# Expert activations of a two-layer decoder trunk: one 512-column and one 256-column matmul per K chunk, halves joined by adding DMAs

## The chip, the cores and the metric

One core of one Trainium2 chip runs the whole kernel. The metric is the device time of one execution in microseconds (us). The median of three runs of the kernel before is 2028.8 us (2027.66 to 2029.06).

## What is computed

The trunk has two layers over 256 tokens of width 1024. Layer 0 mixes tokens with a state-space block, layer 1 with attention; after each mixer comes a layer norm, a product-key expert block (PEER), another layer norm and a gated embedding add. The change touches only the expert block, which the reference writes as a gather:

```
u_g = u[expert]
v_g = v[expert]
act = jax.nn.gelu(jnp.einsum('td,thkd->thk', xb, u_g).astype(f32))
return jnp.einsum('thk,thkd->td', (gate * act).astype(v_g.dtype), v_g)
```

There are 16,384 experts per layer, `u` and `v` hold one row of 1024 numbers for each, and every token picks 128 of them (8 heads, 16 each). All data are float32.

## The kernel before, in words

The kernel does not gather. For each layer it computes the activation of **every** expert for every token, multiplies it by a gate that is zero for experts that a token did not pick, and multiplies the result by `v`. The 16,384 experts are handled as 128 groups of 128; the code calls a group `e`, and from here on "expert" means such a group.

**Precision.** The matmuls of the experts take operands in a rounded float32 format (float32r). So each operand is split into a high part (a cast on ScalarE, ACT) and a low part (the difference, on VectorE, DVE), and each product is made of three: high·high, high·low and low·high (`SPLIT`, L29). `split` (L112) is the pair of instructions, L113 the cast and L114 the difference.

**Weights.** `chunk` (L117) loads one 128x1024 float32 tile of 512 KB into a `raw` buffer by a DMA issued from SyncE (SP, L124), and splits it into an `hl` tile. There are three `raw` buffers (L110) and four `hl` buffers (L120).

**The u stage** (`expert_in`, L796). `stationary` (L140) goes over eight K chunks of 128. For each it calls `mm3` (L136): three matmuls whose stationary operand is a 128x128 piece of the weights (high, high, low) and whose moving operand is 256 tokens of the transposed activations `xT` (high, low, high). So an expert is 24 matmuls of 256 columns. Two experts share one 128x512 bank of PSUM (tag `mm`, two banks, L98), and after the second ACT applies Gelu to the whole bank and writes it to SBUF (L803), into one of four `act` tiles of 32 experts each.

**The v stage** (`expert`, L860). The gated activations of an expert are split into `w`, its `v` tile into `hl`, and 12 matmuls of 512 columns (2 token blocks x 2 column halves x 3) add into four PSUM banks (tag `acc`, four banks, L101) over all 128 experts.

**Order of the work.** The instruction order on each engine is fixed when the program is built. `weave` (L40) spreads a list of side steps over a list of main steps, so that VectorE's routing and gating work lies between the loads of the experts. In a layer the u stage runs with three kinds of company: two experts among the queries (L865 to L871); experts 2 to 71 with `route`, the top-16 searches and lookups on VectorE (L873); experts 72 to 127 with the first half of the gating (L874). The v stage runs its first 62 experts with the second half of the gating, `second` (L876). The gating builds one-hot tiles (L815 to L821), multiplies them on TensorE (L830) and multiplies the result into `act` (`weigh`, L837). Towards the end of the v stage the 512 KB tiles of the next projection (`w_pg`) are loaded among the experts (L891).

GpSimd (POOL) has almost nothing to do and issues no DMA.

Of the kernel before, what the change touches and what calls it, by code (L numbers as in the profile page):

```python
# [7 lines left out]
F32 = mybir.dt.float32  # L8
# [3 lines left out]
AF = mybir.ActivationFunctionType  # L12
OP = mybir.AluOpType
# [4 lines left out]
P = 128  # L18
T = 256
D = 1024  # L20
KD = D // P
# [36 lines left out]
class Net:  # L58
# [48 lines left out]
        return self.ps.tile([P, 512], F32, tag="aux", bufs=2, name=self.name("aux"))  # L107

    def raw(self):
        return self.stream.tile([P, 1024], F32, tag="raw", bufs=3, name=self.name("raw"))  # L110

    def split(self, hi, lo, src, lo_on=None):  # L112
        a = self.nc.scalar.copy(hi, src)  # L113
# [16 lines left out]
    def plain(self, src):  # L130
        raw = self.raw()
        dma = self.nc.sync.dma_start(raw, src)
        self.pace.marks = (dma.ins,)
        return raw
# [5 lines left out]
    def stationary(self, out, hl, m=P):  # L140
        for k in range(KD):
            self.mm3(out, lambda a: hl[:, a, k * m:(k + 1) * m], lambda b: self.xT[:, b, k, :],
                     k == 0, k == KD - 1)

    def moving(self, out, hl, xk, first, last, c=slice(0, 512)):
        for k in range(2):
            self.mm3(out, lambda a: xk(a, k), lambda b: hl[:, b, k * 512 + c.start:k * 512 + c.stop],
                     first and k == 0, last and k == 1)
# [4 lines left out]
    def load_xT(self, j):  # L153
        raw = self.xT32[:, 2 * j:2 * j + 2, :].rearrange("p k t -> p (k t)")
        self.nc.sync.dma_start(raw, self.dram["xT"][j])
        f = lambda a: self.xT[:, a, 2 * j:2 * j + 2, :].rearrange("p k t -> p (k t)")
        self.split(f(0), f(1), raw)
# [179 lines left out]
    def tl(self, shape, tag, bufs, dt=F32):  # L337
        return self.pool.tile(shape, dt, tag=tag, bufs=bufs, name=self.name(tag))
# [319 lines left out]
    def peer(self, i):  # L658
        nc, dram = self.nc, self.dram
        with self.tc.tile_pool(name=f"peer{i}", bufs=1) as pool:  # L660
            self.pool = pool
            tl = lambda shape, dt, tag, bufs=1: self.tl(shape, tag, bufs, dt)
# [130 lines left out]
            act = {}  # L793
            cur = {}

            def expert_in(e):  # L796
                if e % 32 == 0:
                    act[e // 32] = tl([P, 32, T], F32, f"act{e // 32}")
                if e % 2 == 0:
                    cur["ph"] = self.mm().rearrange("p (e t) -> p e t", e=2)  # L800
                self.stationary(cur["ph"][:, e % 2], self.chunk(dram["u"][i, e]))
                if e % 2:
                    nc.scalar.activation(act[e // 32][:, e % 32 - 1:e % 32 + 1, :], cur["ph"], AF.Gelu_apprx_tanh)  # L803

            gw = {}

# [33 lines left out]
            def gating(half):  # L840
                steps = []
                for tg in range(0, 32, 2):
                    steps += [lambda tg=tg: pick(half, tg), lambda tg=tg: pick(half, tg + 1),
                              lambda tg=tg: spread((tg, tg + 1)),
                              lambda tg=tg: weigh(half, tg), lambda tg=tg: weigh(half, tg + 1)]
                return steps
# [3 lines left out]
            def expert_load(e, w=None, hl=None):  # L850
                w = tl([P, 2, T], F32R, "w", 3) if w is None else w
                self.split(w[:, 0, :], w[:, 1, :], act[e // 32][:, e % 32, :])
                return w, self.chunk(dram["v"][i, e], hl=hl)

            def expert_out(e, w, hl, tb):
                for h in range(2):
                    self.mm3(accs[tb][h], lambda a: w[:, a, tb * P:(tb + 1) * P],
                             lambda b: hl[:, b, h * 512:(h + 1) * 512], e == 0, e == 127)

            def expert(e):  # L860
                w, hl = expert_load(e)
                for tb in range(2):
                    expert_out(e, w, hl, tb)

            for hc in range(19):  # L865
                if hc < 16:
                    query(hc)
                elif hc < 18:
                    expert_in(hc - 16)
                if hc >= 3:  # L870
                    score(hc - 3)  # L871
            first, second = gating(0), gating(1)
            self.weave([lambda e=e: expert_in(e) for e in range(2, 72)], route)  # L873
            self.weave([lambda e=e: expert_in(e) for e in range(72, 128)], first)  # L874
            accs += self.accs()
            self.weave([lambda e=e: expert(e) for e in range(62)], second)  # L876
            self.weave([lambda e=e: expert(e) for e in range(62, 90)], [])
            res = tl([P, 4, 2, D], F32, "act1")
            x, gb0, gb1, pp = (res[:, k] for k in range(4))
# [163 lines left out]
```

## Time and profile before

| | |
|---|---|
| median of 3 runs | 2028.8 us |
| profiled execution, its own time | 2027.79 us |
| span of the profile (first to last instruction) | 2026.0 us |
| granted TensorE clock | 1.00 throughout |
| TensorE, weight loads | 1817.5 us busy (90%), 14,706 of them |
| DMA queue of SP | 367.29 MB, 56.1% of 16 engines |
| u stage of layer 0 / layer 1 | about 283 to 660 us / 1248 to 1625 us |
| v stage of layer 0 / layer 1 | about 660 to 1023 us / 1625 to 1990 us |

How to read it: all durations in the groups come from that one profiled execution, which took 2027.79 us by its own clock, 1.8 us more than the span. A line such as `L113 ACT CAST hl<-raw ... x626 | 654.8, 1047` says that the instructions of line 113 on ACT were 626, busy for 654.8 us in all, 1047 ns each on average. A matmul's duration is its whole way through the array, and neighbours overlap, so the time that one costs is read from how many fit in a stretch of the chain of waits. In the rows by windows, each row is a stretch of the span, then its length, then the busy time of each engine in it with the number of instructions, the granted clock, and the DMA engines' busy share and rate.

### The profile page before, as it was taken

Reading aid. Unit: us, or ns where it says so; the run is one execution under the profiler, and the core shown is the slowest. Engines: PE = TensorE matmul, PEld = TensorE weight load, DVE = VectorE, ACT = ScalarE, POOL = GpSimd, SP = SyncE. Lnnn points to the kernel's source line nnn. Section 1 sums busy time; section 2 is a strip of 40 time slices with the busy share of each in tenths; the row PEclk is TensorE's granted clock in tenths of the full one; section 3 lists DMA queues with packets and bytes.
Section 4 is the critical chain, followed back from the end, with each engine's and each line's share of the span. In section 5 each row is a group of like instructions: output and inputs, shape, how many; then the busy total and the mean of one; then the engine's idle time right before and its main releaser. Section 6 shows DMA issues by size and latency. Waiting matters only on the chain.

```text
span 2026.0 us, 36796 instructions
## 1 busy us (share of the span) xinstructions
PE 2001.7 (99%) x14706; PEld 1817.5 (90%) x14706; DVE 1553.3 (77%) x3050; ACT 1010.6 (50%) x1472; POOL 26.4 (1%) x31
## 2 busy tenths in 40 slices
PE   9999999999999999999999999999999999999998
PEld 8888899999999888888879889999999988888887
DVE  8786659997777988866665655999787888986665
ACT  6754544455444444445545654445544444445553
POOL 0001000000000000000000000000000000000000
PEclk9999999999999999999999999999999999999999
DMA  7446655555555555666745555555555555566672
GB/s 270 156 133 197 210 174 181 179 184 184 159 173 161 176 167 187 226 209 201 235 138 177 177 179 165 186 179 187 175 161 175 159 178 175 178 214 221 201 227 83
DMA packets 102732, 369.64 MB, mean 182 GB/s; under 512 B 11392, under 2 KB 12320, under 8 KB 100896
## 3 DMA queue, kind: packets, MB, share of 16 engines
q1 hardware_dynamic: 102560, 367.29, 56.1%
q8 instruction: 115, 1.88, 0.4%
q14 instruction: 57, 0.47, 0.1%
HBM read 360.92 MB, written 6.32 MB: 181 GB/s over the span
## 4 chain that ended last, share of the span: by engine, by line
PE 79%; issue 8%; DMA 5%; DVE 5%; ACT 2%; POOL 1%; SPq 0%; POOLq 0%; ACTq 0%
PE mm L138 42%; PE acc L138 31%; DMA raw<-in_v 3%; PE aux L830 3%; DVE hl L114 2%; ACT hl L113 1%; DVE cv_y L351 1%; DMA raw<-in_w_pg 1%; PE aux L689 1%; PE aux L456 0%; DMA raw<-in_w_xbc 0%; PE mm L166 0%; PE mm L371 0%; DMA raw<-in_w_q 0%; POOL sq L477 0%
## 5 line engine op out<-in xcount | busy, mean ns | idle before, releaser
L138 PE MATMUL mm<-xT,hl 128*128 128x256 f32 x8112 | 1003.4, 284 | 1.8 <-DVE hl L114 1.1
L138 PEld LDWEIGHTS mm<-xT,hl 128*128 128x128 f32 x8112 | 981.5, 192 | 6.3 <-issue 2.0
L114 DVE TENSOR_TENSOR hl<-raw,hl 128x1024 fp32r<-128x1024 f32 x624 | 758.6, 1221 | 282.3 <-ACT hl L113 280.2
L113 ACT CAST hl<-raw 128x1024 fp32r<-128x1024 f32 x626 | 654.8, 1047 | 291.6 <-PE mm L138 174.2
L138 PE MATMUL acc<-hl,w 128*128 128x512 f32 x3024 | 697.5, 391 | 1.5 <-DVE hl L114 0.7
L138 PEld LDWEIGHTS acc<-hl,w 128*128 128x128 f32 x3024 | 564.7, 188 | 120.7 <-DVE hl L114 2.3
L113 ACT CAST w<-act 128x256 fp32r<-128x256 f32 x252 | 101.9, 406 | 269.0 <-PE acc L138 261.1
L803 ACT ACTIVATE act<-mm 128x512 f32<-128x512 f32 x128 | 76.5, 598 | 227.6 <-PE mm L138 227.4
L114 DVE TENSOR_TENSOR w<-act,w 128x256 fp32r<-128x256 f32 x252 | 106.0, 421 | 43.7 <-ACT w L113 42.9
L837 DVE SCALAR_TENSOR_TENSOR act<-aux,act 128x256 f32<-128x256 f32 x256 | 90.5, 416 | 26.0 <-PE aux L830 26.0
L821 DVE TENSOR_TENSOR a<-oh,r 128x512 f16<-128x512 f16 x256 | 96.3, 417 | 0.0
L815 DVE TENSOR_TENSOR oh<-iota,r 128x1024 f16<-128x1024 f16 x128 | 87.2, 682 | 0.0
L830 PEld LDWEIGHTS <-oh 128*128 128x128 f16 x2048 | 63.3, 98 | 9.7 <-issue 8.4
L830 PE MATMUL aux<-a,oh 128*128 128x64 f16 x2048 | 70.9, 193 | 0.0
L817 DVE TENSOR_TENSOR oh<-iota,r 128x512 f16<-128x512 f16 x128 | 53.3, 417 | 0.0
L138 PE MATMUL acc<-hl,nhl 128*128 128x512 f32 x192 | 49.2, 407 | 0.0
L138 PEld LDWEIGHTS acc<-hl,nhl 128*128 128x128 f32 x192 | 34.8, 188 | 9.8 <-issue 1.0
L138 PE MATMUL acc<-act,xT 128*128 128x512 f32 (+1 forms) x186 | 40.8, 373 | 0.0
L138 PEld LDWEIGHTS acc<-act,xT 128*128 128x128 f32 x186 | 32.2, 189 | 5.6
L351 DVE SCALAR_TENSOR_TENSOR cv_y<-cv_raw,params,cv_y 128x253 f32<-128x253 f32 (+2 forms) x72 | 34.4, 486 | 2.3 <-ACT cv_y L348 1.8
L727 DVE MAX8 act<-act 128x8 f32<-128x128 f32 (+1 forms) x96 | 32.1, 334 | 2.3
L114 DVE TENSOR_TENSOR act<-raw,act 128x1024 fp32r<-128x1024 f32 x16 | 19.6, 1226 | 16.3 <-ACT act L113 16.2
(213 smaller groups left out, 1048.7 us busy)
## 6 DMA issues: line engine op xcount, KB each, us to landing
raw<-in_u SPq DMA_DIRECT2D x256, 512.0 KB, 3.6
raw<-in_v SPq DMA_DIRECT2D x256, 512.0 KB, 4.3
raw<-in_w_q SPq DMA_DIRECT2D x32, 512.0 KB, 4.5
raw<-in_w_xbc SPq DMA_DIRECT2D x24, 512.0 KB, 3.7
raw<-in_w_z SPq DMA_DIRECT2D x16, 512.0 KB, 3.5
raw<-in_w_so SPq DMA_DIRECT2D x16, 512.0 KB, 4.4
raw<-in_w_pg SPq DMA_DIRECT2D x16, 512.0 KB, 4.5
raw<-in_w_qk SPq DMA_DIRECT2D x16, 512.0 KB, 3.9
```

Of the source, the lines that this page charges most:

```text
L113: a = self.nc.scalar.copy(hi, src)
L114: b = (lo_on or self.nc.vector).tensor_tensor(lo, src, hi.bitcast(F32), op=OP.subtract)
L138: self.nc.tensor.matmul(out, lhs(a), rhs(b), start=start and i == 0, stop=stop and i == 2)
L351: nc.vector.scalar_tensor_tensor(y[:, d:], raw[:, :T - d], w(k), y[:, d:], op0=OP.mult, op1=OP.add)
L689: nc.tensor.matmul(pss[:, tb], q[:, tb * P:(tb + 1) * P], keys[:, hc, :], start=True, stop=True)
L727: nc.vector.max(vals[:, 8:], src)
L803: nc.scalar.activation(act[e // 32][:, e % 32 - 1:e % 32 + 1, :], cur["ph"], AF.Gelu_apprx_tanh)
L815: nc.vector.tensor_tensor(pairs(oh2), every(self.iota, P), twins(i2T, P), op=OP.is_equal)
L817: nc.vector.tensor_tensor(pairs(oh1), every(self.iota[:, 64 * half:64 * half + 64], 64), twins(i1T, 64), op=OP.is_equal)
L821: nc.vector.tensor_tensor(pairs(a2[:, k]), pairs(oh1), twins(g2[:, k], 64), op=OP.mult)
L830: nc.tensor.matmul(pg[:, t, :], oh2[:, t], a2[:, k, t], start=k == 0, stop=k == 1)
L837: nc.vector.scalar_tensor_tensor(v, pg[:, :, 32 * a:32 * a + 32].rearrange("p t e -> p e t"), 2.0 ** -12, v, op0=OP.mult, op1=OP.mult)
```

## The change

For each K chunk of an expert, two matmuls take the place of three. The first has the high part of the weights as its stationary operand and 512 moving columns: the high parts of the 256 tokens and then their low parts, which lie 8 KB apart in each partition of `xT`. The second has the low part of the weights and 256 columns, the high parts, and adds into the first half of the bank. So the bank holds high·high + low·high in its first half and high·low in its second. An expert has a bank of its own, of tag `acc`.

ACT copies the first half into `act` and the second into a new tile `low` (three buffers of two experts). After each second expert GpSimd issues a DMA that adds `low` (256 KB, from SBUF) onto the two experts in `act` (SBUF). Gelu is applied in place in SBUF to four experts at a time, 128x1024, and is ordered on ACT behind the copies of the expert that ends the next four; the last four follow inside the v stage, as the fourth side step of `second`. `raw` gets a fourth buffer, and the space that is reserved in SBUF for the descriptors of GpSimd's DMAs is set to 4096 bytes per partition.

```diff
     def raw(self):
-        return self.stream.tile([P, 1024], F32, tag="raw", bufs=3, name=self.name("raw"))
+        return self.stream.tile([P, 1024], F32, tag="raw", bufs=4, name=self.name("raw"))
...
+    def halves(self, out, hl):
+        o = out.rearrange("p (b t) -> p b t", b=2)
+        for k in range(KD):
+            c = slice(k * P, (k + 1) * P)
+            self.nc.tensor.matmul(o, hl[:, 0, c], self.xT[:, :, k, :], start=k == 0, stop=False)
+            self.nc.tensor.matmul(out[:, :T], hl[:, 1, c], self.xT[:, 0, k, :], start=False, stop=k == KD - 1)
...
+            def gelu(e):
+                x = act[e // 32][:, e % 32:e % 32 + 4, :].rearrange("p e t -> p (e t)")
+                nc.scalar.activation(x, x, AF.Gelu_apprx_tanh)
+
             def expert_in(e):
                 if e % 32 == 0:
                     act[e // 32] = tl([P, 32, T], F32, f"act{e // 32}")
                 if e % 2 == 0:
-                    cur["ph"] = self.mm().rearrange("p (e t) -> p e t", e=2)
-                self.stationary(cur["ph"][:, e % 2], self.chunk(dram["u"][i, e]))
+                    cur["low"] = tl([P, 2, T], F32, "low", 3)
+                pe = self.acc()
+                self.halves(pe, self.chunk(dram["u"][i, e]))
+                nc.scalar.copy(act[e // 32][:, e % 32, :], pe[:, :T])
+                copied = nc.scalar.copy(cur["low"][:, e % 2, :], pe[:, T:]).ins
                 if e % 2:
-                    nc.scalar.activation(act[e // 32][:, e % 32 - 1:e % 32 + 1, :], cur["ph"], AF.Gelu_apprx_tanh)
+                    both = act[e // 32][:, e % 32 - 1:e % 32 + 1, :]
+                    nc.gpsimd.dma_start(both, cur["low"], accum_op=OP.add)
+                if e % 4 == 3 and e > 3:
+                    with self.after((copied,)):
+                        gelu(e - 7)
...
             accs += self.accs()
+            second.insert(3, lambda: gelu(124))
             self.weave([lambda e=e: expert(e) for e in range(62)], second)
...
-    nc = bacc.Bacc("TRN2", target_bir_lowering=False, num_devices=1)
+    nc = bacc.Bacc("TRN2", target_bir_lowering=False, num_devices=1, dynamic_dma_scratch_size=4096)
```

## The prediction

> **What bounds the kernel now.** I read the page first, then the chain of waits in order of time, then the stages by windows, then the groups and waits of the u stage.
>
> ```profile
> PE 2001.7 (99%) x14706; PEld 1817.5 (90%) x14706; DVE 1553.3 (77%) x3050; ACT 1010.6 (50%) x1472; POOL 26.4 (1%) x31
> ...
> PE 79%; issue 8%; DMA 5%; DVE 5%; ACT 2%; POOL 1%; SPq 0%; POOLq 0%; ACTq 0%
> ```
>
> TensorE is busy for 99% of the span and carries 79% of the chain that ended last. A busy matmul is not yet a matmul that costs time, so the next view is the chain in order of time, in pieces of so many matmuls (start, length, what):
>
> ```profile
> 283.66 198.71 PE mm L138 x1656
> ...
> 846.38 119.82 PE acc L138 x528
> ...
> 1248.07 198.71 PE mm L138 x1656
> ```
>
> The first and third rows are 69 experts of the u stage of each layer without a break: 198.71 us / 1656 = 120.0 ns for a matmul of 256 columns. The second is 44 experts of the v stage: 119.82 / 528 = 226.9 ns for 512 columns. Doubling the columns adds 106.9 ns, so 256 columns cost 106.9 ns of streaming and each matmul about 13.1 ns besides, whatever its size. In these stretches TensorE never waits, so the u stage is as long as its matmuls. The rows of the routing and gating stretches say how far the others are from taking over:
>
> ```profile
> core 0: us, PE busy (x) PEld busy (x) DVE busy (x) ACT busy (x) POOL busy (x), PEclk, DMA share, GB/s
> ...
> 283.00:482.00 199.00, 199.00 (x1661) 199.00 (x1661) 182.18 (x494) 100.25 (x118) 0.00 (x0) 1.00 0.58 183
> 482.00:660.00 178.00, 178.00 (x1857) 177.31 (x1856) 139.92 (x248) 74.42 (x91) 0.00 (x0) 1.00 0.53 166
> ...
> 293.00:373.00 80.00, 80.00 (x669) 80.00 (x668) 74.75 (x242) 35.51 (x43) 0.00 (x0) 1.00 0.59 185
> 373.00:433.00 60.00, 60.00 (x502) 60.00 (x501) 59.28 (x160) 26.87 (x31) 0.00 (x0) 1.00 0.55 176
> 433.00:463.00 30.00, 30.00 (x252) 30.00 (x251) 27.72 (x53) 22.27 (x27) 0.00 (x0) 1.00 0.64 194
> ```
>
> VectorE is the one to watch: 182.18 of 199 us beside the routing, and 59.28 of 60 us in its densest part. ACT, the DMA engines and, above all, POOL (no instruction) have room.
>
> **The change part by part.**
>
> *TensorE.* Per K chunk 3 x 120.0 = 360.0 ns become 226.9 + 120.0 = 346.9 ns: the columns stay the same, 768, and one matmul's fixed 13.1 ns goes. Per expert 8 x 13.1 = 0.105 us, for 256 experts 2048 x 13.1 ns = 26.8 us. All of it lies on the path. The new matmul's moving operand comes in two runs of 256, which no matmul of this kernel does now; the bounds are 226.9 ns (the row of 512 columns in one run) and 2 x 120.0 = 240.0 ns (as if each run were a matmul of its own), that is 26.8 us or nothing. I take 226.9, as the row nearest in columns and in instructions; the other end is a rival.
>
> [...]
>
> *ACT.* The groups that give its prices (busy, mean ns, then idle before and what ended it); the last two are of the size of the new Gelu and of the new copies:
>
> ```profile
> L114 DVE TENSOR_TENSOR hl<-raw,hl 128x1024 fp32r<-128x1024 f32 x69 | 83.9, 1215 | 11.7 <-ACT hl L113 11.2 <-PE mm L138 0.5
> ...
> L113 ACT CAST hl<-raw 128x1024 fp32r<-128x1024 f32 x69 | 72.1, 1045 | 42.5 <-PE mm L138 38.7 <-DMA raw<-in_u 3.8
> L803 ACT ACTIVATE act<-mm 128x512 f32<-128x512 f32 x35 | 20.9, 597 | 54.6 <-PE mm L138 54.5
> L755 ACT COPY act<-act 128x1024 f16<-128x1024 f16 x8 | 8.0, 1044 | 0.0
> ...
> L690 ACT COPY act<-aux 128x256 f32<-128x256 f32 x2 | 0.7, 370 | 0.0
> ```
>
> For two experts ACT now does 0.60 us of Gelu and 2 x 1.05 of casts, 2.69 us in 5.76. After: four copies of 0.37, two casts, and half a Gelu of 128x1024, priced like the cast and L755 at 1.05: 1.48 + 2.09 + 0.52 = 4.09 us in 5.55. It fits, off the path. What it moves is the time at which the high part of a later expert is cast. The row of L113 shows that cast waiting for TensorE for 38.7 us: it is issued when an expert's matmuls end and free one of four `hl` tiles, so TensorE has three experts in hand, 8.3 us, while cast (1.05) and difference on VectorE (1.22) follow. The copies delay it by 0.74 us, every fourth time by a Gelu more. Cover remains, so I cost it at nothing; without that cover it would be 0.74 to 1.8 us per expert.
>
> One stretch is tight. From 433 to 463 us ACT is busy for 22.27 of 30 us. In the same experts, 10.4 of them, it gets 5.2 x (4.09 - 2.69) = 7.3 us more, 29.6 in the 28.9 us that TensorE then takes. Just before it, from 373 to 433 us, VectorE has 59.28 us of work where TensorE will take 60 x 346.9/360 = 57.8. Together that is 0.7 + 1.5 = 2.2 us per layer by which helpers fall behind; three experts in hand can absorb it, down to nothing lost. Bounds: 0 to 2.2 us per layer; I take 1, so 2 us.
>
> *The wait that is added.* Gelu of four experts stands on ACT's queue and waits for the adding DMA; behind it are the next copies and casts, for them VectorE's differences, and for these TensorE. It stands behind the copies of the expert that ends the next four, so the younger of the two DMAs has 4 x 2.78 = 11.1 us from its issue. No DMA of this kernel adds or is issued by POOL. The nearest rows are moves of 256 KB (KB each, then us from issue to landing); the load of an expert and the whole queue stand beside them:
>
> ```profile
> raw<-in_u SPq DMA_DIRECT2D x256, 512.0 KB, 3.6
> ...
> q1 hardware_dynamic: 102560, 367.29, 56.1%
> ...
> act<-in_keys SPq DMA_DIRECT2D x8, 256.0 KB, 5.2
> ...
> x_d<-xn SPq DMA_DIRECT2D x4, 256.0 KB, 2.6
> ```
>
> They land 2.6 to 5.2 us after issue. Even twice the longer is 10.4 us, inside the 11.1, and behind these come the 8.3 us that TensorE has in hand; so I cost the wait at nothing at both ends, as long as the DMA engines keep up (a rival). POOL's queue holds nothing else in these stages (0.00, x0), and SP's queue is not touched by the adds. The engine time: 367.29 MB are 56.1% of 2026 us, so all 16 engines together move 323 GB/s, and a plain 256 KB costs 0.81 us. Loads take 2 x 524 KB / 323 = 3.25 us of the 5.55 us of two experts; 2.3 us are free, 2.8 times a plain copy.
>
> *The last four.* Their Gelu comes in the v stage, where ACT reaches it as soon as the fourth expert's cast is issued, about when the u stage ends; its adding DMA lands 0.74 us of copies and 2.6 to 5.2 us later, and 8.2 us of v matmuls are in hand. The v stage's four banks are now those of the last four experts of the u stage; the last of the four is first written 9 x 0.227 = 2.0 us into the stage and its copies take 0.74. I take 0.5 us per layer for the seam, 1 us in all; bounds 0 and 2.
>
> *The fourth `raw` buffer.* It matters where a load ends a wait, at the end of the v stage with the extra `w_pg` tiles:
>
> ```profile
> 966.00:1064.00 98.00, 96.42 (x436) 78.38 (x435) 63.03 (x88) 47.82 (x67) 2.05 (x3) 1.00 0.59 183
> ...
> 1909.00:2007.00 98.00, 95.68 (x420) 76.97 (x419) 63.77 (x88) 51.36 (x71) 1.09 (x2) 1.00 0.59 183
> ...
> 968.98 4.68 DMA raw<-in_v
> 976.03 4.31 DMA raw<-in_v
> ```
>
> The last two rows are from the chain of waits: there the path runs from load to load, about 7 us for three buffers. But TensorE idles in these two stretches for only 1.58 + 2.32 = 3.9 us, part of it behind a layer norm. I take 2 us of gain, bounds 0 and 4.
>
> *Sum.* -26.8 - 2 + 2 + 1 = -25.8 us against the profiled execution's 2027.79: 2002.0. That execution lies 1.0 us below the median of the runs, so the forecast for the median is **2003 us**, 1.3% less.
>
> **The rivals.**
>
> *The DMA engines become the bound (slower).* [...] If it costs twice a plain copy, 1.6 us, it fits in the 2.3 us that are free. It decides from 5.76 - 3.25 = 2.5 us on, 3.1 times a plain copy: then two experts take longer than the 5.76 us of now, loads come late and ACT stands at Gelu or TensorE at a bank. At four times, 3.25 us, two experts take 6.5 us: 128 x 0.74 = 95 us more, about 2124 us. For it: an addition is done on the way and nothing here shows its rate. Against it: the margin of nearly three. Chance 0.14.
>
> *VectorE and ACT take over beside the routing (half a gain).* For it: 59.28 of 60 us and ACT's 29.6 in 28.9. In the row of L114 above VectorE stands waiting for ACT's cast for 11.2 us of that stage, with the routing queued behind it. If the later casts double these, VectorE needs 182.18 + 11.7 + 11.2 = 205 us for a stage that TensorE would do in 192: the stage ends 13 us later than forecast, less what 8.3 us in hand cover, 5 us per layer. 2003 + 10 = 2013 us. Against it: a VectorE that is behind no longer waits for casts. Chance 0.12.
>
> *Nothing is saved on TensorE.* If each of the two runs costs as much as a matmul, the 26.8 us stay: 2028.8 + 1, about 2030 us, no change. Against it: nothing in the trace points to a cost of a second run. Chance 0.06.
>
> **How the numbers follow.** Forecast 0.68, helpers 0.12, nothing saved 0.06, DMA bound 0.14. The forecast's own range is 1994 to 2009: below, the stalls at nothing (-3), all of the 3.9 us (-2) and another 4 us where the chain's 5% of DMA waits lie in other stages; above, their upper bounds (2.4 more at the routing, 1 at the seam, 2 for `raw`). Two of ten may be left out, so the range reaches over the helpers' case and as far beyond it, to 2023. About 0.2%, 4 us, is what a measurement of this kernel can tell from no change. Faster: 0.68 + 0.12 = 0.80; same 0.06; slower 0.14.
>
> **What would show it.** In the chain after, the u stage stands as unbroken pieces of 16 matmuls per expert, 2.78 us each instead of 2.88; 1656 matmuls of two layers' routing stretch become 1104 in about 191.5 us each. The new 512-column form steps at 227 ns; 240 would prove the third rival. Adding DMAs land within 5 us or so, DMA share in the u stage rises from 0.58 to 0.75 or 0.9, and Gelu waits for none of them; a Gelu that waits for a DMA and a share near 1 would prove the first. Casts of `raw` at the end of the v stage should wait less for loads. The forecast is wrong if the u stages don't shrink by 13 us each.

## The result and the profile after

The kernel after takes 1997.4 us (median of 6 runs, 1996.32 to 1998.53), the kernel before 2028.2 us beside it (6 runs, 2026.55 to 2029.35): a ratio of 0.9848, interval 0.9837 to 0.9859. That is 30.8 us less, where the forecast had 25.8. The profiled execution after took 1996.32 us by its own clock, the lowest of its six, with a span of 1994.4 us against 2026.0. The total is near the forecast. Two of its terms are not, as the stages show.

From the page of the kernel after: busy time, the two DMA queues with packets, MB and share, the shares of the chain, three groups of ACT and POOL, and two rows of DMA issues.

```profile
PE 1977.0 (99%) x12658; PEld 1706.0 (86%) x12658; DVE 1549.8 (78%) x3050; ACT 1138.1 (57%) x1920; POOL 135.4 (7%) x159
...
q1 hardware_dynamic: 102560, 367.29, 55.4%
q0 software_dynamic: 18432, 33.56, 9.9%
...
PE 85%; issue 7%; DVE 5%; ACT 2%; POOL 1%; DMA 1%; SPq 0%; POOLq 0%; ACTq 0%; DVEq 0%
...
L814 ACT COPY act<-acc 128x256 f32<-128x256 f32 x256 | 96.2, 376 | 254.2 <-PE acc L150 254.2
...
L815 ACT COPY low<-acc 128x256 f32<-128x256 f32 x256 | 98.2, 384 | 0.0
...
L805 ACT ACTIVATE act<-act 128x1024 f32<-128x1024 f32 x64 | 69.0, 1078 | 0.8 <-DMA act<-low 0.8
...
raw<-in_u SPq DMA_DIRECT2D x256, 512.0 KB, 4.4
...
act<-low POOLq DMA_DIRECT2D x128, 256.0 KB, 5.5
```

TensorE has the 2048 matmuls less (14,706 - 12,658). Gelu (L805) stood idle for an adding DMA for 0.8 us in the whole run. An adding DMA lands 5.5 us after its issue and costs 9.9% x 1994.4 / 128 = 1.54 us of all 16 engines, 1.9 times the 0.81 us worked out for a plain copy. What in it costs the time is not shown. DMA has gone from 5% of the chain to 1%; the forecast's term for it was 2 us.

Where the time went is read from landmarks in the chain of waits (start, length, what). Before: the first layer norm, the first v matmuls of layer 0, their last two pieces, the next layer norm, and the same for layer 1.

```profile
212.38 3.53 DVE xn L189 x2
...
663.39 8.19 PE acc L138 x36
...
1023.56 6.87 PE acc L138 x29
1030.87 1.39 PE acc L138 x6
...
1178.70 2.86 DVE x L189
...
1627.80 8.19 PE acc L138 x36
...
1996.72 1.39 PE acc L138 x6
```

After:

```profile
208.82 3.55 DVE xn L196 x2
...
649.77 8.19 PE acc L138 x36
...
832.76 181.01 PE acc L138 x798
1014.21 1.39 PE acc L138 x6
...
1160.65 2.92 DVE x L196
...
1600.99 8.20 PE acc L138 x36
...
1784.00 181.01 PE acc L138 x798
1965.45 1.39 PE acc L138 x6
```

The differences of these starts, in us:

| stretch | before | after | change |
|---|---|---|---|
| start to first layer norm | 212.4 | 208.8 | -3.6 |
| norm to v stage, layer 0 (holds the u stage) | 451.0 | 440.9 | -10.1 |
| v stage, layer 0 | 367.5 | 364.4 | -3.0 |
| attention, to the norm of layer 1 | 147.8 | 146.4 | -1.4 |
| norm to v stage, layer 1 (holds the u stage) | 449.1 | 440.3 | -8.8 |
| v stage, layer 1 | 368.9 | 364.5 | -4.5 |
| rest | 29.3 | 29.0 | -0.3 |

The u stages gave 18.8 us, not 26.8 (23.8 with the stalls that were forecast); the other stages, where of the change only the fourth buffer and the last Gelu of a layer lie, gave 12.8 us, not 2. The last 798 matmuls of each v stage now run without a break, at 181.01 / 798 = 226.8 ns. Two questions follow: why a buffer was worth so much, and where 8 us of the u stages went.

### The profile page after: what moved, and what is told of

Its sections match the earlier page's. It is cut to its first block, busy times and chain, and to the rows that moved or that the text cites. A ratio compares the mean times of both kernels' runs of the same rounds, so it can differ in the third digit from the quotient of the medians.

```text
span 1994.4 us, 33756 instructions
## 1 busy us (share of the span) xinstructions
PE 1977.0 (99%) x12658; PEld 1706.0 (86%) x12658; DVE 1549.8 (78%) x3050; ACT 1138.1 (57%) x1920; POOL 135.4 (7%) x159
## 4 chain that ended last, share of the span: by engine, by line
PE 85%; issue 7%; DVE 5%; ACT 2%; POOL 1%; DMA 1%; SPq 0%; POOLq 0%; ACTq 0%; DVEq 0%
PE acc L138 38%; PE acc L149 21%; PE acc L150 11%; PE mm L138 8%; PE aux L848 3%; DVE hl L114 1%; PE aux L696 1%; PE mm L378 1%; ACT hl L113 0%; PE aux L463 0%; PE mm L173 0%; DVE act L732 0%; PE mm L291 0%; DVE act L733 0%; DVE act L735 0%
## 5 line engine op out<-in xcount | busy, mean ns | idle before, releaser
L149 PE MATMUL acc<-xT,hl 128*128 128x512 f32 x2048 | 722.4, 397 | 0.0
L150 PE MATMUL acc<-xT,hl 128*128 128x256 f32 x2048 | 573.9, 280 | 0.4 <-DVE hl L114 0.4
L149 PEld LDWEIGHTS acc<-xT,hl 128*128 128x128 f32 x2048 | 384.8, 188 | 88.6
L150 PEld LDWEIGHTS acc<-xT,hl 128*128 128x128 f32 x2048 | 387.4, 189 | 1.1 <-DVE hl L114 1.1
L138 PE MATMUL mm<-xT,hl 128*128 128x256 f32 x1968 | 256.4, 287 | 0.8 <-DVE xT L114 0.7
L138 PEld LDWEIGHTS mm<-xT,hl 128*128 128x128 f32 x1968 | 242.3, 192 | 5.0 <-issue 2.3
L814 ACT COPY act<-acc 128x256 f32<-128x256 f32 x256 | 96.2, 376 | 254.2 <-PE acc L150 254.2
L818 POOL DMA_DIRECT2D act<-low x128 | 110.5, 863 | 758.5 <-ACT low L815 619.4
L815 ACT COPY low<-acc 128x256 f32<-128x256 f32 x256 | 98.2, 384 | 0.0
L805 ACT ACTIVATE act<-act 128x1024 f32<-128x1024 f32 x64 | 69.0, 1078 | 0.8 <-DMA act<-low 0.8
L193 POOL TENSOR_TENSOR ln_s<-ln_s,mhalf 128x1 f32<-128x1 f32 x8 | 4.4, 549 | 874.3 <-DVE ln_s L192 874.3
```

The lines of the kernel that those rows point to most:

```text
L138: self.nc.tensor.matmul(out, lhs(a), rhs(b), start=start and i == 0, stop=stop and i == 2)
L149: self.nc.tensor.matmul(o, hl[:, 0, c], self.xT[:, :, k, :], start=k == 0, stop=False)
L150: self.nc.tensor.matmul(out[:, :T], hl[:, 1, c], self.xT[:, 0, k, :], start=False, stop=k == KD - 1)
L814: nc.scalar.copy(act[e // 32][:, e % 32, :], pe[:, :T])
L815: copied = nc.scalar.copy(cur["low"][:, e % 2, :], pe[:, T:]).ins
L818: nc.gpsimd.dma_start(both, cur["low"], accum_op=OP.add)
```

## The experiments

### raw4_only: the fourth buffer alone

```diff
 (kernel before)
-        return self.stream.tile([P, 1024], F32, tag="raw", bufs=3, name=self.name("raw"))
+        return self.stream.tile([P, 1024], F32, tag="raw", bufs=4, name=self.name("raw"))
...
-    nc = bacc.Bacc("TRN2", target_bir_lowering=False, num_devices=1)
+    nc = bacc.Bacc("TRN2", target_bir_lowering=False, num_devices=1, dynamic_dma_scratch_size=4096)
```

> The kernel before with the fourth raw buffer and the 4096 bytes of descriptor space alone. Theory 1, read from the two traces: the gain of 30.8 us is two gains, about 18.8 us in the two u stages (the matmuls) and about 12.5 us outside them (3.6 before the first norm, 3.0 and 4.5 in the v stages, 1.4 in the attention), and the second comes from the fourth buffer alone. Then this kernel is 12 us faster than the kernel before, ratio 0.994. Theory 2, the sizes of the prediction: the buffer is worth 2 us, at most 4, ratio 0.998 to 0.999, and the rest comes with the new matmuls.

Measured: 2016.2 us (5 runs, 2015.11 to 2016.65), ratio 0.9943, interval 0.993 to 0.9957: 12 us less than before. Its chain at the same landmarks:

```profile
209.16 3.55 DVE xn L189 x2
...
659.44 8.19 PE acc L138 x36
...
842.43 181.01 PE acc L138 x798
1023.88 1.39 PE acc L138 x6
...
1170.14 2.93 DVE x L189
...
1620.68 8.19 PE acc L138 x36
...
1985.12 1.39 PE acc L138 x6
```

The same steps as in the table: -3.2 to the first norm, -0.7, -3.0 in the v stage (364.4), -1.6, +1.4, and -4.5 in the second v stage (364.4). The v stages, the first mixer and the attention come out as in the kernel after to within 0.4 us. So the buffer alone explains what lies outside the u stages, and its gain lies in four stages, of which the prediction had looked at two, the v stages.

### raw3: everything but the fourth buffer

```diff
 (kernel after)
-        return self.stream.tile([P, 1024], F32, tag="raw", bufs=4, name=self.name("raw"))
+        return self.stream.tile([P, 1024], F32, tag="raw", bufs=3, name=self.name("raw"))
```

> The changed kernel with three raw buffers. Theory 1: only the u stages are shorter, by 18 to 19 us together, ratio 0.991. Theory 2: the matmuls give the 26.8 us of the prediction less 2 or 3 of stalls, ratio 0.988. If three buffers are too few for loads beside the adding DMAs, TensorE waits for loads in the u stage and less than 15 us are left.

Measured: 2007.0 us (4 runs, 2003.51 to 2008.25), ratio 0.9894, interval 0.9879 to 0.9909: 21.1 us less than before. The chain of its v stage goes from load to load again. In its profiled execution, the slowest of the four, the u stages (442.7 and 440.5 us between the landmarks) are 16.9 us shorter than before; the two v stages (366.5 and 365.8 us) are 4.1 us shorter, for which the runs show no cause. The total lies between the two theories, and its interval, 18.5 to 24.5 us, does not part them. 12.0 + 21.1 is 2.3 us more than the 30.8 of both; that interval covers this too.

### no_add: without the adding DMAs

```diff
                 if e % 2:
                     both = act[e // 32][:, e % 32 - 1:e % 32 + 1, :]
-                    nc.gpsimd.dma_start(both, cur["low"], accum_op=OP.add)
+                    pass
```

The high·low part stays out of the activations here.

> The changed kernel without the 128 adding DMAs: the high x low part of each activation is computed and copied, but left out of the result. Theory 1: the adds are hidden, so the time is that of the changed kernel within 2 us (about 1997), with the DMA share of the u stage back from 0.8 to 0.6, and the pair of matmuls still at 353 ns in the unbroken stretch. Rival: the adds slow loads or TensorE's reads, and the pair goes to 347 ns: 6 us faster, about 1991.

Measured: 1998.1 us (4 runs, 1996.43 to 1998.97), ratio 0.9857, interval 0.9842 to 0.9872. Without them nothing is gained: the adding DMAs, their wait and their traffic cost nothing that the runs can tell. Nor do they set TensorE's pace. The 512-column matmuls of the u stage alone, from 300 to 400 us (stretch, length, PE, PEld, granted clock, DMA share, GB/s), are as many as in the kernel after, where they are 284 at a DMA share of 0.84:

```profile
300.00:400.00 100.00, 100.00 (x285) 53.22 (x284) 1.00 0.55 184
```

### add_twice: a second adding DMA for each pair of experts

```diff
                     nc.gpsimd.dma_start(both, cur["low"], accum_op=OP.add)
+                    if e == 1:
+                        cur["sink"] = tl([P, 2, 2, T], F32, "sink", 1)
+                        nc.vector.memset(cur["sink"], 0.0)
+                    nc.gpsimd.dma_start(cur["sink"][:, e // 2 % 2], cur["low"], accum_op=OP.add)
```

The second goes onto a tile that nothing reads; `dynamic_dma_scratch_size` is 2048 instead of 4096.

> The changed kernel with a second adding DMA of the same size after each, onto a tile that is not read (descriptor space 2048 bytes to make room). In the changed kernel q0 takes 9.9% of 16 engines over the span for 128 adds, 1.54 us each of all 16 engines, 1.9 times a plain copy, and the engines are busy for 0.82 of the u stage. Theory: the second add needs 1.54 us more in the 5.7 us of two experts, 0.27 of the engines, and 0.82 + 0.27 is over 1: the engines become the bound and the u stages grow by about a tenth, 40 to 80 us in all, 2040 to 2080. Rival: the busy share overstates what is used, loads and adds overlap, and the time stays within 5 us of 1997.

Measured: 1998.8 us (4 runs, 1996.63 to 1999.61), ratio 0.9855, interval 0.984 to 0.987. Rows by windows over the u stage of layer 0 (stretch, length, busy time and instructions of PE, PEld, DVE, ACT and POOL, granted clock, DMA share, GB/s):

```profile
279.00:470.00 191.00, 190.90 (x1082) 165.45 (x1082) 176.72 (x495) 134.44 (x235) 59.84 (x68) 1.00 1.03 271
470.00:650.00 180.00, 180.00 (x1457) 158.11 (x1457) 145.23 (x259) 109.43 (x198) 50.87 (x58) 1.00 1.00 262
```

The DMA share is 1.03, TensorE idles for 0.1 of 191 us, and from 300 to 400 us it does the same 284 of the 512-column matmuls as in after. So the theory of 40 to 80 us fell, and a share of 1 was no bound here: it sums the time that packets took, 1.03 of the stretch, and the time was 1998.8 us against 1997.4.

### soon: Gelu behind its own four experts, with no hold

```diff
-                if e % 4 == 3 and e > 3:
+                if e % 4 == 3:
                     with self.after((copied,)):
-                        gelu(e - 7)
+                        gelu(e - 3)
...
-            second.insert(3, lambda: gelu(124))
```

> The changed kernel with Gelu of four experts right behind the copies of the last of them, not behind the next four. An adding DMA lands 5.5 us after its issue in the changed kernel. ACT then stands at Gelu for 5 to 6 us every four experts, with the casts of the next experts behind it, while TensorE has three experts, 8.3 us, in hand. If that cover is real, the stand costs little: within 4 us of 1997. If the hold is what makes the change work, TensorE waits 2 us or more every four experts: 64 x 2 = 128 us slower than the changed kernel, about 2125.

Measured: 2024.9 us (10 runs, 2021.48 to 2027.55), ratio 0.9985, interval 0.9976 to 0.9994: 27.5 us more than after, nearly the whole gain, and far from both numbers expected (1997 and 2125). The group of Gelu on its page:

```profile
L805 ACT ACTIVATE act<-act 128x1024 f32<-128x1024 f32 x64 | 67.9, 1061 | 154.7 <-DMA act<-low 154.7
```

ACT waits 154.7 us, and yet most of it is covered; it comes out at a few places. Here is one, in ACT's and then TensorE's timeline:

```profile
435.17 0.31 ACT L752 ACTIVATE act<-act 128x128 f32<-128x128 f32 x1 [3.07 <-DVE act L751]
...
438.72 1.06 ACT L113 CAST hl<-raw 128x1024 fp32r<-128x1024 f32 x1
439.67 2.00 ACT L762 COPY act<-act 128x1024 f16<-128x1024 f16 x2
444.37 1.28 ACT L805 ACT_TABLE_LOAD   x1 [2.71 <-DMA act<-low]
445.67 1.06 ACT L805 ACTIVATE act<-act 128x1024 f32<-128x1024 f32 x1
...
447.68 2.02 ACT L113 CAST hl<-raw 128x1024 fp32r<-128x1024 f32 x2
```

```profile
445.15 0.28 PE L150 MATMUL acc<-xT,hl 128*128 128x256 f32 x1
448.80 0.50 PE L149 MATMUL acc<-xT,hl 128*128 128x512 f32 x1 [3.38 <-ACT hl L113]
```

Between two casts of `hl`, at 438.72 and 447.68 us, ACT does 2.00 us of the routing's copies, waits 2.71 us for the DMA, loads its table (`ACT_TABLE_LOAD`, 1.28 us), does Gelu (1.06 us) and makes four copies (0.35 to 0.40 us each). TensorE has less in hand here than three experts: from the end of the first cast (439.78) to its stop (445.43) it works for 5.65 us, two experts; ACT had already stood 3.07 us for VectorE at 435.17. And the break costs more than its 3.4 us; the same kernel by windows:

```profile
445.00:450.00 5.00, 0.93 (x4) 0.28 (x2) 1.52 (x4) 4.99 (x10) 0.86 (x1) 1.00 0.04 9
450.00:455.00 5.00, 4.94 (x20) 4.21 (x20) 4.82 (x6) 5.00 (x9) 0.86 (x1) 0.66 0.91 243
455.00:460.00 5.00, 5.00 (x31) 4.34 (x30) 3.71 (x6) 1.88 (x3) 0.00 (x0) 1.00 0.99 297
```

Behind it, from 450 to 455 us, the granted clock is 0.66, an estimated 1.7 us lost (0.34 x 5). Counted in 512-column matmuls, soon does 94 from 440 to 480 us and after 114: 20 pairs of 346 ns, about 7 us. The second place in layer 0 is the start of the v stage, where TensorE waits 2.68 us for a cast of `w`, after ACT stood 7.43 us at Gelu. The two make up most of the 11.2 us by which this u stage is longer than in after (452.2 us against 440.9 between the landmarks). In layer 1, 10.8 us longer, TensorE waits 4.4 us for a cast, and from 1400 to 1420 us soon does 36 of the 512-column matmuls, 56 to 58 in each of the like stretches ahead of it. So the hold behind the next four is what makes the added wait free (0.8 us of waiting in after, 154.7 here).

### contig, by_form, kick, by_form_kick: where 8 us of the u stages went

In the kernel after, the starts of matmuls in TensorE's timeline show the price of a K chunk, that is of one 512-column matmul and one of 256. Seven starts of the 512-column form in a stretch of routing, first and last:

```profile
335.90 0.40 PE L149 MATMUL acc<-xT,hl 128*128 128x512 f32 x1
...
338.02 0.40 PE L149 MATMUL acc<-xT,hl 128*128 128x512 f32 x1
```

Eight in the gating:

```profile
599.71 0.39 PE L149 MATMUL acc<-xT,hl 128*128 128x512 f32 x1
...
602.13 0.39 PE L149 MATMUL acc<-xT,hl 128*128 128x512 f32 x1
```

2.12 / 6 = 353 ns in the first place, 2.42 / 7 = 346 ns in the second, at the same granted clock of 1.00 and with the same instructions. The forecast had 346.9. The slower pace holds from the start of the unbroken stretch, near 279 us, to a short stall (0.2 us) behind VectorE near 443 us, in layer 1 from 1225 to 1394 us; from the stall on it is the faster one. 164 us / 353 = 464 K chunks at 6.4 ns more are 3.0 us, in both layers about 6 of the missing 8 us. The other 2 us are a remainder that no run takes apart.

*contig* lays `xT` out as [K chunk, high and low, tokens], so that the 512 columns are one run (all users of `xT` follow):

```diff
-        self.xT = self.state.tile([P, 2, KD, T], F32R, name="xT")
+        self.xT = self.state.tile([P, KD, 2, T], F32R, name="xT")
...
-            self.nc.tensor.matmul(o, hl[:, 0, c], self.xT[:, :, k, :], start=k == 0, stop=False)
+            self.nc.tensor.matmul(out, hl[:, 0, c], self.xT[:, k].rearrange("p b t -> p (b t)"), start=k == 0, stop=False)
```

> The changed kernel with xT laid out by K chunk first, so that the 512 moving columns of a chunk are one run. The pair of matmuls takes 353 ns in the unbroken stretch of the changed kernel's u stage, and the steps of 512 columns in a row were 230.6 ns where the v stage has 226.9. Theory 1 now (the second run costs some 4 to 6 ns): the pair falls to 347 ns everywhere, 5 to 6 us faster than the changed kernel, about 1991.5. Rival (a phase of weight loads and matmuls that the sequence falls into, whatever the operand): no change, 1997.

Measured: 1998.3 us (5 runs, 1997.42 to 1999.43), ratio 0.9851, interval 0.9837 to 0.9864.

*by_form* puts an expert's eight 512-column matmuls first and its eight of 256 after them:

```diff
             self.nc.tensor.matmul(o, hl[:, 0, c], self.xT[:, :, k, :], start=k == 0, stop=False)
+        for k in range(KD):
+            c = slice(k * P, (k + 1) * P)
             self.nc.tensor.matmul(out[:, :T], hl[:, 1, c], self.xT[:, 0, k, :], start=False, stop=k == KD - 1)
```

> The changed kernel with the order of the matmuls within an expert changed: first the eight of 512 columns, then the eight of 256. The trace of the changed kernel shows a pair at 353 ns in the unbroken stretch of the u stage and at 347 ns after a break. Theory 1: the slow pace is a matter of the alternation of the two sizes, and runs of one size step at 227 and 120 ns: 347 ns throughout, about 6 us faster than the changed kernel, 1991. Rival: the two runs of the moving operand cost it, and steps of 512 columns stay at 230 ns or more: no faster than 1997.

Measured: 1994.6 us (4 runs, 1994.0 to 1994.82), ratio 0.9838, interval 0.9822 to 0.9853.

*kick* adds one matmul of another kind, which nothing reads, ahead of expert 6 of each layer, to break the pattern once:

```diff
                 pe = self.acc()
+                if e == 6:
+                    nc.tensor.matmul(self.aux()[:, :64], self.iota, self.iota[:, :64], start=True, stop=True)
                 self.halves(pe, self.chunk(dram["u"][i, e]))
```

> The changed kernel with one small float16 matmul (64 columns into a spare bank, never read) ahead of expert 6 of each layer. In the changed kernel the pair takes 353 ns up to the first short stall, at 443 and 1394 us, and 347 ns after it. Phase theory: the small matmul breaks the pattern as that stall did, and the pair takes 347 ns from expert 6 on: 3 us per layer, 1991.5. Theory of the second run: nothing changes, 1997.

Measured: 1995.0 us (4 runs, 1994.75 to 1995.71), ratio 0.9834, interval 0.9819 to 0.9849.

The 512-column matmuls of the u stage alone, counted in the 100 us from 300 to 400: one row each of after, contig, by_form and kick, in this order (stretch, length, PE, PEld, granted clock, DMA share, GB/s).

```profile
300.00:400.00 100.00, 100.00 (x284) 53.25 (x283) 1.00 0.84 229
```

```profile
300.00:400.00 100.00, 100.00 (x284) 53.18 (x283) 1.00 0.83 229
```

```profile
300.00:400.00 100.00, 71.57 (x288) 51.37 (x287) 1.00 0.85 231
```

```profile
300.00:400.00 100.00, 100.00 (x289) 54.03 (x289) 1.00 0.85 232
```

100 us hold 284 K chunks in after (352 ns) and the same in contig: the two runs of the operand are not the cost of the slower pace, and that theory of mine fell. One foreign matmul, at expert 6 some 10 us earlier, makes them 289 (346 ns), and nothing else was changed. So the same alternating pair ran at two paces, 352 and 346 ns, at a granted clock of 1.00, and in these runs the faster one followed a break of its rhythm: the stall of 0.2 us in after, the foreign matmul in kick. What in the chip holds the slower one, the runs do not show. In by_form the starts of the groups give 1.84 us for eight of 512 columns (230 ns each) and 0.95 us for eight of 256 (119 ns). So the 512-column form stays 3 ns above the 226.9 of the v stage; whether its two runs cost that is open, because by_form was not run with the layout of contig.

Not all of the faster pace reaches the end. What TensorE waited for from 279 to 470 us, in after and in kick (in total, times, longest):

```profile
PE acc L150 <- DVE hl L114: 0.2, 1, 0.2
```

```profile
PE acc L150 <- DVE hl L114: 1.3, 2, 0.7
```

In kick TensorE gains almost 3 us in the stretch and then waits 1.1 us more for VectorE: there the helpers do become the bound for a moment, as the prediction's term for them says. by_form gives a part back elsewhere: from 480 to 640 us, beside the gating, it runs 414 of the 512-column matmuls where after runs 417.

*by_form_kick* has both edits.

> The kernel after with both earlier edits: an expert's eight matmuls of 512 columns first and its eight of 256 after them, and one matmul of 64 columns of fp16, never read, ahead of expert 6 of each layer. The median with the order alone was 1994.6 us, with the 64-column matmul alone 1994.98, after 1997.42. Theory 1, the slower pace belongs to the alternation of the two forms, which the order removes: nothing more comes, 1994 to 1995 us, and 512 columns behind 512 still take 226 to 236 ns, 230.6 on average. Theory 2, the order has a slower pace of its own that a break ends too: 512 behind 512 goes to 226.9 ns, the routing stretch gets 57 x 7 x 3.7 ns = 1.5 us per layer shorter, 1992 us. Theory 3, VectorE sets the end of the routing stretch already in both: the pace may rise, the time stays at 1994 to 1995 and TensorE idles more at its end.

Measured: 1994.4 us (5 runs, 1994.31 to 1995.21), ratio 0.9836, interval 0.9823 to 0.985. The 512-column matmuls from 300 to 400 us are 288, as in by_form: the slower pace (284 in after) came only with the two forms alternating, and with the order changed a break brought nothing more. All three medians (by_form, kick, by_form_kick) lie 2.4 to 3.0 us below after, and none of their 13 runs overlaps with its six. So they beat both kernels, after by 0.12 to 0.15%; the intervals of their ratios still overlap with that of after.

### raw5: a fifth buffer

```diff
-        return self.stream.tile([P, 1024], F32, tag="raw", bufs=4, name=self.name("raw"))
+        return self.stream.tile([P, 1024], F32, tag="raw", bufs=5, name=self.name("raw"))
...
-                    cur["low"] = tl([P, 2, T], F32, "low", 3)
+                    cur["low"] = tl([P, 2, T], F32, "low", 2)
```

> The kernel after with a fifth raw buffer; to make room, low has two buffers instead of three. The fourth buffer alone was worth 12 us, in the first mixer and at the end of the v stages. Theory 1, four buffers end the waits of the v stages (181 us of matmuls without a break in the chain after), and what is left is a few us of loads in the first mixer, 1% of the chain: 1994 to 1998 us, the chain's DMA share 0 to 1%. Theory 2, every buffer more moves loads ahead and shortens more stages: 1988 us or less. Were two buffers of low too few, the copies into low would wait for the adding DMA and the u stages would get longer.

Measured: 2000.7 us (4 runs, 1998.18 to 2002.29), ratio 0.9862, interval 0.9847 to 0.9877. That is above both theories. Its last 798 matmuls of a v stage take the same 181.01 us: four buffers are enough there. The copies into `low`, which has two buffers here, wait 1.5 us in all for the adding DMAs, and the u stage of layer 1 is 1.4 us longer. The first mixer is worse in the profiled execution, which is the slowest of the four: the first layer norm comes at 213.82 us instead of 208.82. The order of the instructions there differs from that of after. By windows:

```profile
185.00:190.00 5.00, 2.17 (x11) 1.48 (x10) 4.35 (x9) 2.00 (x4) 2.79 (x2) 0.91 0.86 273
190.00:195.00 5.00, 4.92 (x12) 3.86 (x13) 2.60 (x8) 1.22 (x4) 0.00 (x0) 0.50 0.43 158
195.00:200.00 5.00, 5.00 (x21) 4.02 (x20) 1.48 (x2) 2.10 (x2) 0.00 (x0) 0.91 0.21 59
```

TensorE idles for 2.8 us from 185 to 190 us, in breaks of 0.68 and 2.23 us, and from 190 to 195 us the granted clock is 0.50: of the 5 us, up to an estimated 3.4 (0.09 + 0.50 + 0.09 of 5 us each) are the clock's. Why the clock fell, the runs do not show.

## Why the prediction was right or wrong

*TensorE.* The step that failed is the price of the pair, 226.9 + 120.0 = 346.9 ns from the rows of like matmuls behind one another. Alternating, the pair takes 353 ns in the long unbroken stretch of each layer and 346 elsewhere: 6 us of 26.8. The bounds (226.9 or 240 ns) were drawn around the operand's two runs, and contig shows that those cost nothing in the alternation. So the rival "nothing is saved on TensorE" named the wrong danger, though about a quarter of the saving went.

*ACT's and VectorE's extra work, and the seam.* Copies of 376 and 384 ns and a Gelu of 1078 ns are close to what was assumed (370 and 1050). Of the 8 us missing in the u stages 6 are the pace; about 2 are left for the helpers, the seam and whatever else, where the prediction had 3; this remainder was not measured by itself. The rival that VectorE and ACT take over, 13 us per layer less 8.3 us of cover, did not come. Its mechanism shows only when TensorE is quicker, in kick, and is worth about 1 us per layer.

*The added wait.* Nothing, as said (0.8 us of ACT's idle time; no_add gains nothing). But one of the two reasons given for it is weak. The prediction put 8.3 us in hand behind the 11.1 us of the hold, and soon shows that those three experts alone do not carry it: 27.5 us come back. The hold carries it: the adding DMAs landed 3.3 to 8.1 us after their issue, inside the 11.1.

*The fourth `raw` buffer.* This step failed most: -2 us, bounds 0 to 4, against -12 measured alone. It fails at "TensorE idles in these two stretches for only 1.58 + 2.32 = 3.9 us". Idle time was the wrong ruler, since a busy matmul is not one that goes at its pace, which the prediction itself says at its start. Counting matmuls gives the size: in the v stage of layer 0 before, 528 of the last 798 end at 966.20 us, and the other 270 end at 1023.56 + 6.87 = 1030.43 us, in 64.2 us; at 226.9 ns they are 61.3. That is 3.0 us, the measured gain of the stage, where the idle time shows 1.6. In layer 1, 432 end at 1908.86 and the other 366 at 1996.28 us, in 87.4 us instead of 83.0: 4.4 us, against a measured 4.5. And it fails by looking at the v stages alone: the first mixer (3.2 us in raw4_only) and the attention (1.6 us) held most of the rest. The 5% of DMA in the chain, some 100 us in which loads were the last to end, was the hint; it served for the low bound only.

*The DMA engines as the bound.* Twice a plain copy was the guess for an adding DMA, 1.9 times is measured (1.54 against 0.81 us). The point from which it decides was wrong: the prediction has 3.1 times a plain copy, from a sum of busy shares. add_twice asks for an estimated 2 x 1.54 = 3.1 us per pair of experts, 3.8 times, and loses nothing that its runs can tell.

*The sum.* -25.8 forecast and -31.5 between the own times of the two profiled executions. The u stages gave 5 us less than the terms for them (-26.8 + 2 + 1 = -23.8 against -18.8), the buffer 10 us more: two errors that partly cancel, so that the total came out so near was luck. The prediction named a sign by which it would be wrong, u stages that don't shrink by 13 us each. They shrank by 10.1 and 8.8 us: by that sign the forecast of the u stages failed. (The sign was stricter than the sum, whose terms leave 11.9 us for each u stage.) The forecast was right in its direction and its range, and less so in its reasons.

## What to carry to other kernels

Price what a late load costs by counting the matmuls of the stretch at their undisturbed pace, in every stage where a load stands in the chain, and not by TensorE's idle time; one more buffer, 12 us here, may be worth more than its idle time promises (3.9 us). A wait for a DMA on ACT, with casts queued behind it, was free here with a hold of an estimated 11.1 us ahead of it, longer than the DMA's landing (3.3 to 8.1 us), and cost 27.5 us, nearly the whole gain, without one. Prices from runs of like matmuls did not hold for an alternation here (346.9 ns against 353): read the pace again from starts, and try another order.

## What the runs showed of the hardware

- The same alternation of a 512- and a 256-column matmul ran at 353 or at 346 ns per pair at a granted clock of 1.00; behind one foreign 64-column matmul (kick) 100 us of the stretch held 289 pairs instead of 284.
- The DMA engines' busy share reached 1.03 (add_twice) at 1998.8 us, against 1997.4 at 0.84; an adding DMA of 256 KB within SBUF took 1.54 us of all 16 engines, 1.9 times the 0.81 us worked out for a plain copy.
- TensorE stood for 2.8 us in raw5 (breaks of 0.68 and 2.23 us) and for 3.38 us in soon, and the 5 us behind had a granted clock of 0.50 (190 to 195 us) and 0.66 (450 to 455 us). With what followed, the stretch cost about 5 us in raw5 and 7 in soon, about twice the break.
